# Feed-forward block of an encoder layer: block pairs gated as (i, i+11), right-operand sums of the down product made at gating, and a rebuilt buffer and load plan for the down product

## The chip, the cores and the metric

One Trainium2 chip, one core. The metric is the device time of one execution in microseconds (us). Three runs of the kernel before took 1331.19, 1335.35 and 1338.98 us; the median is 1335.35 us. The profiled execution is a run of its own, with its own time.

The engines are TensorE (PE, with its weight loads listed as PEld), VectorE (DVE), ScalarE (ACT), GpSimd (POOL) and SyncE (SP), which here only issues transfers. Each engine works through its own list of instructions in order. An instruction that waits holds up everything behind it on its engine, and a transfer that waits holds up those behind it on the queue that issues it.

## The reference, cut to what matters

The kernel computes one encoder layer on 1024 rows of width 1024: an SSD group and a chunked attention group side by side, an output projection, then a gated feed-forward part, and a last norm. The change touches the feed-forward part and the last norm:

```
h   = rmsnorm(x) * (1 + sc_f) + sh_f
u   = causal_dwconv3(h @ w_up)            # 1024 x 5632
g, v = split(u, 2)                        # 1024 x 2816 each
x   = x + g_f * ((silu(g) * v) @ w_down)  # 2816 -> 1024
out = rmsnorm(x) * final_norm_w
```

All of it is float32. The kernel splits each float32 operand into a high and a low part and multiplies three times: high by high, high by low, low by high.

## The kernel before

The 2816 channels of the feed-forward part are 22 blocks of 128. Both matrix products are done by a seven-product scheme for two by two blocks (Strassen's, in Winograd's form), which replaces eight block products by seven at the cost of sums of operands. The products are called P1, P2, P3, Q4, Q5, Q6 and Q7.

**Up product and gating.** A `Unit` (L838 to L902) is one channel block, with its g and its v half. The loop at L938 takes two units at a time, 2q and 2q+1, in 11 rounds (KH = 11). `Unit.__init__` queues the loads of its slice of `w_up` into `ya` or `xs`. `sums` (L844) makes the sums of the weights on DVE. `prep` splits two weight blocks at once through `wsplit` (L818): ACT writes the high part (L66), DVE the low part (L69), both into a buffer of a ring of five (`ring`, L810). `product` runs four steps of three matmuls (`mm3`, L55 to L58) into a PSUM bank of tag X, Y or Z, and `post` empties the bank. `conv` (L889) is the causal convolution: a scaled copy on ACT (L892) and two multiply-adds on DVE (L894). `finish` (L897) does the convolution of the g half, the silu on ACT (L900), the product on DVE (L901), and stores the gated block of 128 channels by 1024 rows into the DRAM tensor `gd`, from ACT's queue (L902).

**Down product.** The tensor `gd` is the right operand and `w_down` the left one. Each is seen as two by two blocks: channel blocks 0 to 10 and 11 to 21 (index 1 and 2), and two halves of 512 rows or columns. So `b11` is blocks 0 to 10 and rows 0 to 511, `b12` the same blocks and rows 512 to 1023, `b21` and `b22` the same halves of blocks 11 to 21; `a11` and so on are the blocks of `w_down`. Two channel blocks at a time are a "pair" m, six pairs per product, the last of one block only (`kn`, L967). `load_pair` (L970) queues a transfer of a pair on SP. `operands` (L1000) makes the sums of a product's operands on DVE through `add` (L995), ten of them for each m over the seven products. `split_pair` (L1022) splits both operands, and `step` (L1026) runs 4 times `mm3`, one for each of four tiles `st` of 128 rows: 12 matmuls for one channel block. The product P1 writes banks d, Q6 banks e, and so on; the order is P1, Q6, Q5, Q7, P3, Q4, P2.

The down stage has a pool of buffers of its own, `dp`, which is opened after those of the up stage are closed, and so lies in the memory that they held. a11, a21, a22, b11, b12 and b22 each have a buffer for each m; a12 and b21 share two buffers (tag `st`) and are loaded for each product anew. `add_x1` (L1042) fetches a tile of the residual `x1d` into one of two buffers, `gate` (L1047) multiplies by the gate row and adds it, and `final` (L1051) does the last norm of four halves of rows and the stores. The last three channel blocks of P2 are kept back and done tile by tile (L1117), so that a tile's norm can run beside the next tile's matmuls.

**What sets the order.** The program is written in one order, but a planner puts the instructions of each engine in the order in which its own model of their times makes them ready; where several are ready, the earlier written goes first. The waits between engines are put in by the framework. A buffer is handed on when all users of the tile that held it are through. The last round of the up stage (q = 10) is not finished in the loop: `finish` of its two units, blocks 20 and 21, is written after the first splits of P1 (L1064 to L1068).

Of the kernel before, what the change touches and what calls it, by code (L numbers as in the profile page):

```python
# [45 lines left out]
def tile_block(ctx: ExitStack, tc: tile.TileContext, x, crep, pk, w_ada, w_first, w_ft, w_z,  # L46
# [13 lines left out]
    def split(hi, lo, src, ehi, elo, scale=None):  # L60
        if scale is not None:
            A.activation(hi, src, AF.Copy, scale=scale)
            V.scalar_tensor_tensor(lo, src, scale, f32(hi), op0=ALU.mult, op1=ALU.subtract)
            return
        if ehi is A:
            A.activation(hi, src, AF.Copy)  # L66
        else:
            ehi.tensor_copy(hi, src)
        elo.tensor_tensor(lo, src, f32(hi), ALU.subtract)  # L69
# [645 lines left out]
    gd = dram.tile([NF, P, S], F32, name="gd")  # L715
# [55 lines left out]
    def h_new(pool, n):  # L771
        hb_[n] = [pool.tile([P, 4, 512], F32R, name=n + p) for p in "hl"]
# [45 lines left out]
    def wsplit(src, n=2):  # L818
        w = ring()[:, :, 0:n, :]
        split(w[:, 0], w[:, 1], src, A, V)  # L820
        return w

    fp_ = []
# [14 lines left out]
    class Unit:  # L838
        def __init__(self, i):
            self.i, self.b, self.ps, self.w, self.done = i, (ya, xs)[i % 2], {}, {}, set()  # L840
# [25 lines left out]
        def post(self, p, ps):  # L866
# [14 lines left out]
            elif p == "Q4":  # L881
                V.tensor_tensor(self.v[:, 0:512], ps, self.v[:, 0:512], ALU.subtract)  # L882
                self.a = a_tile()
# [13 lines left out]
        def finish(self):  # L897
# [4 lines left out]
            nc.scalar.dma_start(gd[self.i], a[:, 1, :])  # L902

    units = [Unit(0), Unit(1)]
# [7 lines left out]
    hc2 = es_h.enter_context(tc.tile_pool(name="hc2", bufs=1, side="right", reuse_waits="tile"))  # L912
    for n in ("t3", "t4", "t1", "b22", "t2"):
        h_new(hc2, n)
# [22 lines left out]

    for q in range(KH):  # L938
        if q > 0:
            units = [Unit(2 * q), Unit(2 * q + 1)]  # L940
# [4 lines left out]
        for n, p in enumerate(order):  # L945
# [5 lines left out]
            for u in units:  # L951
                u.product(p)
        if q < KH - 1:
            for u in units:
                u.finish()
    es_f.close()
    es_h.close()
    es_y.close()


    dp = ctx.enter_context(tc.tile_pool(name="dp", bufs=1, side="right", reuse_waits="tile"))
    ps4 = ctx.enter_context(tc.tile_pool(name="ps4", bufs=1, space=PSUM, reuse_waits="tile"))
    NM = (KH + 1) // 2
    res = {}
    BLK = {"11": (0, 0), "12": (0, 1), "21": (1, 0), "22": (1, 1)}

    def kn(m):  # L967
        return min(2, KH - 2 * m)

    def load_pair(n, m, tag=None):  # L970
        i, j = BLK[n[1:]]
        src = w_down if n[0] == "a" else gd
        if n[0] == "a":
            i, j = j, i
            i, j = (0, 1)[n[2] == "2"], (0, 1)[n[1] == "2"]
        k0 = i * KH + 2 * m
        t = dp.tile([P, kn(m) * 512], F32, tag=tag or f"{n}_{m}", bufs=2 if tag else 1, name=n)
        t = t.rearrange("p (k c) -> p k c", c=512)
        nc.sync.dma_start(t, src[k0:k0 + kn(m), :, halves[j]].rearrange("k p c -> p k c"))
        return t  # L980

    def res_load(names, ms=range(NM)):
        for m in ms:
            for n in names:
                res[n, m] = load_pair(n, m)

    def sm(m):
        t = dp.tile([P, 1024], F32, tag="sm", bufs=2, name="sm")[:, 0:kn(m) * 512]
        return t.rearrange("p (k c) -> p k c", c=512)

    def bank(t="d"):
        return ps4.tile([P, 512], F32, tag=t, bufs=4, name="dn")

    def add(o, a, b, op=ALU.add):
        V.tensor_tensor(o, a, b, op)  # L995
        return o

    sub = ALU.subtract

    def operands(p, m):  # L1000
        r = lambda n: res[n, m]
        if p == "P1":
            return r("a11"), r("b11")
        if p == "Q6":
            add(r("a11"), r("a11"), r("a21"))
            add(r("b11"), r("b11"), r("b12"), sub)
            return add(sm(m), r("a11"), r("a22")), add(sm(m), r("b11"), r("b22"))
        if p == "P2":
            return load_pair("a12", m, "st"), load_pair("b21", m, "st")
        if p == "Q7":  # L1010
            return r("a11"), add(r("b12"), r("b12"), r("b22"), sub)
        if p == "Q5":
            return add(r("a21"), r("a21"), r("a22")), r("b11")
        if p == "Q4":
            t = load_pair("b21", m, "st")
            add(t, t, r("b22"), sub)
            return r("a22"), add(t, t, r("b11"), sub)
        t = load_pair("a12", m, "st")
        add(t, t, r("a22"))
        return add(t, t, r("a11")), r("b22")  # L1020

    def split_pair(p, m):  # L1022
        a, b = operands(p, m)
        return wsplit(a, kn(m)), wsplit(b, kn(m))

    def step(ps, ab, k, sts, start):  # L1026
        a, b = (t[:, :, k % 2, :] for t in ab)
        for st in sts:
            c = slice(st * P, (st + 1) * P)
            mm3(ps[st], b[:, 0, c], b[:, 1, c], a[:, 0, :], a[:, 1, :], start and k == 0,  # L1030
                k == KH - 1, not start)

    def product(p, ps, start, ready=()):
        for m in range(NM):
            ab = ready[m] if m < len(ready) else split_pair(p, m)
            for k in range(2 * m, 2 * m + kn(m)):
                step(ps, ab, k, R4, start)

    def xt_():
        return dp.tile([P, 512], F32, tag="xt", bufs=2, name="xt")  # L1040

    def add_x1(t, st, dh):  # L1042
        x = xt_()
        nc.sync.dma_start(x, x1d[st * P:(st + 1) * P, halves[dh]])
        V.tensor_tensor(t, t, x, ALU.add)

    def gate(t, src, st, dh):  # L1047
# [125 lines left out]
```

## Time and profile before

| | |
|---|---|
| median of three runs | 1335.35 us (1331.19 to 1338.98) |
| profiled execution: its time, its span | 1335.92 us, 1334.2 us |
| PE busy, matmuls | 1216.5 us, 5818 |
| DVE busy, instructions | 991.9 us, 1516 |
| ACT busy, instructions | 550.1 us, 900 |
| last matmul of the up product starts | 1051.13 us |
| first matmul of the down product starts | 1063.22 us |
| last group of matmuls of the down product starts | 1317.95 us |

The profile counts a matmul as busy from its start to its modelled end, and matmuls overlap in the pipeline; so the starts tell more than the busy time. A row of a timeline gives start, duration, engine, line, operation, and output from inputs; in brackets stands the idle time of the engine before it and what ended it. A row of a group gives count, busy time and mean duration, then the idle time before its members. Rows of a table of stretches give for each engine the busy time and the count, then the granted clock of TensorE (1.00 is full speed), the share of the transfer engines and GB/s.

### The profile page before, as it was taken

Reading aid. Unit: us, or ns where it says so; the run is one execution under the profiler, and the core shown is the slowest. Engines: PE = TensorE matmul, PEld = TensorE weight load, DVE = VectorE, ACT = ScalarE, POOL = GpSimd, SP = SyncE. Lnnn points to the kernel's source line nnn. Section 1 sums busy time; section 2 is a strip of 40 time slices with the busy share of each in tenths; the row PEclk is TensorE's granted clock in tenths of the full one; section 3 lists DMA queues with packets and bytes.
Section 4 is the critical chain, followed back from the end, with each engine's and each line's share of the span. In section 5 each row is a group of like instructions: output and inputs, shape, how many; then the busy total and the mean of one; then the engine's idle time right before and its main releaser. Section 6 shows DMA issues by size and latency. Waiting matters only on the chain.

```text
span 1334.2 us, 15392 instructions
## 1 busy us (share of the span) xinstructions
PE 1216.5 (91%) x5818; PEld 995.9 (75%) x5818; DVE 991.9 (74%) x1516; ACT 550.1 (41%) x900; POOL 105.7 (8%) x114
## 2 busy tenths in 40 slices
PE   5999999999999699997799999999999696998884
PEld 4777887788788587775688888888888574886763
DVE  7727566765998877658799887877896689549875
ACT  4525554653233523237344444343344332433332
POOL 1300111001201422110000000000000000000001
PEclk9999998999999999997899999999999797998997
DMA  9601110002745221121122221222220392003264
GB/s 338 218 0 50 33 36 32 27 17 81 257 154 187 96 64 34 62 95 64 63 93 89 87 73 61 77 89 95 95 96 32 137 378 84 0 28 106 80 199 156
DMA packets 50393, 132.23 MB, mean 99 GB/s; under 512 B 4880, under 2 KB 5008, under 8 KB 50320
## 3 DMA queue, kind: packets, MB, share of 16 engines
q1 hardware_dynamic: 44848, 115.53, 25.9%
q10 hardware_dynamic: 5472, 15.73, 3.0%
q8 instruction: 45, 0.74, 0.2%
q14 instruction: 28, 0.23, 0.1%
HBM read 110.79 MB, written 20.45 MB: 98 GB/s over the span
## 4 chain that ended last, share of the span: by engine, by line
PE 67%; DVE 17%; DMA 8%; ACT 3%; issue 2%; POOL 1%; SPq 0%; DVEq 0%; ACTq 0%
PE uY L56 4%; PE uY L57 4%; PE uY L58 4%; DMA b<-gd 3%; PE dn L58 3%; PE uX L56 3%; PE dn L56 3%; PE dn L57 3%; PE uX L57 3%; PE uX L58 3%; PE acc L56 3%; PE acc L57 3%; PE uZ L57 3%; PE uZ L56 3%; PE acc L58 3%; PE uZ L58 3%
## 5 line engine op out<-in xcount | busy, mean ns | idle before, releaser
L56 PE MATMUL dn<-w 128*128 128x512 f32 x308 | 122.8, 413 | 31.4 <-ACT w L66 25.7
L57 PE MATMUL dn<-w 128*128 128x512 f32 x308 | 121.8, 410 | 1.3 <-DVE w L69 1.3
L58 PE MATMUL dn<-w 128*128 128x512 f32 x308 | 108.4, 404 | 6.9 <-DVE w L69 6.9
L56 PEld LDWEIGHTS dn<-w 128*128 128x128 f32 x308 | 61.2, 200 | 47.8 <-ACT w L66 28.8
L66 ACT ACTIVATE w<-ya 128x1024 fp32r<-128x1024 f32 (+1 forms) x44 | 41.8, 949 | 97.4 <-PE uY L58 88.9
L58 PEld LDWEIGHTS dn<-w 128*128 128x128 f32 x308 | 60.2, 197 | 22.1 <-DVE w L69 9.4
L57 PEld LDWEIGHTS dn<-w 128*128 128x128 f32 x308 | 61.4, 200 | 15.2 <-DVE w L69 2.0
L66 ACT ACTIVATE w<-b 128x1024 fp32r<-128x1024 f32 (+1 forms) x36 | 35.5, 987 | 87.5 <-PE dn L58 58.9
L69 DVE TENSOR_TENSOR w<-b,w 128x1024 fp32r<-128x1024 f32 (+1 forms) x36 | 40.8, 1132 | 40.0 <-ACT w L66 40.0
L753 POOL TENSOR_TENSOR st<-st,mhalf 128x1 f32<-128x1 f32 x16 | 11.8, 739 | 735.5 <-DVE st L752 735.3
L69 DVE TENSOR_TENSOR pt<-tp,pt 128x512 fp32r<-128x512 f32 (+2 forms) x72 | 42.2, 595 | 27.7 <-ACT pt L66 27.6
L66 ACT ACTIVATE w<-xs 128x1024 fp32r<-128x1024 f32 (+1 forms) x44 | 41.8, 950 | 40.9 <-PE uY L58 33.7
L894 DVE SCALAR_TENSOR_TENSOR a<-cv,pkt,a 128x1023 f32<-128x1023 f32 (+1 forms) x44 | 56.2, 1276 | 1.4 <-ACT a L892 1.3
L66 ACT ACTIVATE pt<-tp 128x512 fp32r<-128x512 f32 (+2 forms) x72 | 36.7, 523 | 45.0 <-PE tp L349 16.0
L56 PE MATMUL s<-hth,wh 128*128 128x512 f32 x128 | 51.4, 402 | 3.8 <-DVE ct L413 2.3
L894 DVE SCALAR_TENSOR_TENSOR a<-cg,pkt,a 128x1023 f32<-128x1023 f32 (+1 forms) x44 | 54.5, 1277 | 0.0
L882 DVE TENSOR_TENSOR cv<-uY,cv 128x512 f32<-128x512 f32 x22 | 15.1, 687 | 50.4 <-PE uY L58 50.4
L317 DVE CUSTOM_DVE_ANT_0 p<-s,bias 128x640 f32<-128x640 f32 (+4 forms) x64 | 40.3, 649 | 15.9 <-PE tp L352 7.5
L57 PE MATMUL s<-htl,wh 128*128 128x512 f32 x128 | 51.2, 400 | 0.0
L69 DVE TENSOR_TENSOR w<-ya,w 128x1024 fp32r<-128x1024 f32 (+1 forms) x44 | 47.7, 1085 | 4.4 <-ACT w L66 4.4
L58 PE MATMUL s<-hth,wl 128*128 128x512 f32 x128 | 50.8, 397 | 0.0
L69 POOL TENSOR_TENSOR wl<-raw_t,wh 128x1024 fp32r<-128x1024 f32 x14 | 35.0, 2501 | 185.9 <-ACT wh L66 152.5
(334 smaller groups left out, 3629.8 us busy)
## 6 DMA issues: line engine op xcount, KB each, us to landing
mt<-in_w_ada_dram SPq DMA_DIRECT2D x32, 512.0 KB, 4.3
a<-in_w_down_dram SPq DMA_DIRECT2D x25, 512.0 KB, 6.9
b<-gd SPq DMA_DIRECT2D x25, 512.0 KB, 5.2
gd<-a ACTq DMA_DIRECT2D x22, 512.0 KB, 3.0
ya<-in_w_up_dram SPq DMA_DIRECT2D x11, 768.0 KB, 4.1
xs<-in_w_up_dram SPq DMA_DIRECT2D x11, 768.0 KB, 4.8
adat<-in_w_ada_dram SPq DMA_DIRECT2D x16, 512.0 KB, 5.9
raw_t<-in_w_ft_dram SPq DMA_DIRECT2D x14, 512.0 KB, 3.5
```

The costliest lines, as they stand in the source:

```text
L56: T.matmul(ps, lh, rh, start=start, stop=False, skip_group_check=more)
L57: T.matmul(ps, lh, rl, start=False, stop=False, skip_group_check=more)
L58: T.matmul(ps, ll, rh, start=False, stop=stop, skip_group_check=more)
L66: A.activation(hi, src, AF.Copy)
L69: elo.tensor_tensor(lo, src, f32(hi), ALU.subtract)
L317: V.tensor_tensor_reduce(out=dst, in0=src, in1=bsl, scale=-1.0, scalar=3e38, op0=ALU.add, op1=ALU.min, accum_out=nm)
L753: G.tensor_tensor(r, ms, mhalf[:, 0:1], ALU.pow)
L882: V.tensor_tensor(self.v[:, 0:512], ps, self.v[:, 0:512], ALU.subtract)
L894: V.scalar_tensor_tensor(a[:, j:S], c[:, 0:S - j], w[2 - j], a[:, j:S], op0=ALU.mult, op1=ALU.add)
```

## The change

1. The loop takes units q and 11+q together instead of 2q and 2q+1, so that a round has one block of each half of the right operand.
2. `finish` no longer stores the whole block. For the unit of the first half, b11's part is stored ("x"). A new `store_pair` makes the four sums that the seven products need of the right operand, t1 = b11-b12, t3 = b12-b22, t2 = b22+t1 and t4 = b21-t2, by four DVE instructions of 128x512, and stores them from ACT's queue: t1 and t3 (tensor "y", 512 KB) and t2, t4, b21 and b22 (tensor "z", 1 MB).
3. The down stage has no pool of its own. Its buffers are the slots of the up product's operands (`HOME`), each handed over once the operand in it has had its last product; the right operands go round in 14 slots. A queue in the program (`queue`, `pump`) writes a load as soon as its slot's last reader is written, and every load is kept behind the load before it (`issue_after`).
4. The first two pairs of P1 are loaded and split before P3 of the last round; the emptying of P3's banks and `finish` are kept behind those splits. `finish` of block 10 comes after them, and `finish` of block 21 and the last `store_pair` after the split of P1's fourth pair (m = 3).
5. The order of products is P1, Q5, Q6, Q7, Q4, P3, P2. Every product has its own PSUM group, alternately in banks d and e. The left operand's sums are made in place: two for each m in Q5, one in Q6, one in P3. Each is kept behind the low part of the pair three places earlier.
6. `gate` and `final` use parts of `ya` and `xs`; three of the four groups of gates come right after Q6, Q7 and Q4, the fourth with the tail. The last tile's sum is made in `p1` instead of the transfer buffer.

```
+            if self.i < KH:
+                nc.scalar.dma_start(gd["x", self.i // 2][self.i % 2, :, 0], a[:, 1, 0:512])
+    def store_pair(units):
+        q, (a, c) = units[0].i, (u.a for u in units)
+        h0, h1 = halves
+        m, k = q // 2, q % 2
+        V.tensor_tensor(a[:, 0, h0], a[:, 1, h0], a[:, 1, h1], ALU.subtract)
+        V.tensor_tensor(a[:, 0, h1], a[:, 1, h1], c[:, 1, h1], ALU.subtract)
+        nc.scalar.dma_start(gd["y", m][k].rearrange("p a b -> p (a b)"), a[:, 0, :])
+        V.tensor_tensor(c[:, 0, h0], c[:, 1, h1], a[:, 0, h0], ALU.add)
+        V.tensor_tensor(c[:, 0, h1], c[:, 1, h0], c[:, 0, h0], ALU.subtract)
+        nc.scalar.dma_start(gd["z", m][k].rearrange("p a b -> p (a b)"), c.rearrange("p a b -> p (a b)"))
...
+    def load(key, m):
...
+        with tc.issue_after(last_load[0]) if last_load else ExitStack():
+            i = nc.sync.dma_start(t, src.rearrange("k p c -> p k c"))
...
+    def pump():
+        while queue and (queue[0][0] in ("a11", "a21", "a22") or sc[0] % NS not in busy):
+            n, m = queue.pop(0)
+            res[n, m] = load(n, m)
...
+    def down_first():
+        loads(("a11", "b11"), range(NM - 1))
+        loads(("a11",), (NM - 1,))
+        pre = []
+        for m in range(2):
+            a, b = res["a11", m], take("b11", m)
+            pre.append((wsplit(a), wsplit(b)))
+            los.append(last_split[1].ins)
+        return pre
...
-            units = [Unit(2 * q), Unit(2 * q + 1)]
+            units = [Unit(q), Unit(KH + q)]
...
-            for u in units:
-                u.product(p)
+            if p == "P3" and q == KH - 1:
+                pre = down_first()
+            with tc.issue_after(los[0]) if los else ExitStack():
+                for u in units:
+                    u.product(p)
...
+    def add(o, a, b):
+        with tc.issue_after(los[max(0, len(los) - 3)]):
+            V.tensor_tensor(o, a, b, ALU.add)
         return o
...
+        if p == "Q5":
+            add(a11, a11, a21)
+            add(a21, a21, a22)
+        elif p == "Q6":
+            add(a21, a11, a22)
+        elif p in ("P3", "P2"):
+            a = take("a12" + p, m)
+            if p == "P3":
+                add(a, a, a21)
...
+    def late(m):
+        if m == 3:
+            with tc.issue_after(last_split[0].ins), tc.issue_after(last_split[1].ins):
+                units[1].finish()
+                store_pair(units)
+            loads(("a21", "a22", "t1"), range(4, NM))
+            for n in ("t2", "t3", "t4"):
+                loads((n,))
+            loads(("a12P3", "b22"))
+            loads(("a12P2", "b21"))
+            nc.sync.dma_start(gf, gfd)
```

277 lines of the change are left out of this document (153 added, 124 removed).

## The prediction, made before the change was run

> **What bounds the kernel now.** I read the page first, then the stretches from the feed-forward part on, then the groups of the down product, then each engine's timeline there. The page, with TensorE's slices and clock:
>
> ```profile
> span 1334.2 us, 15392 instructions
> ...
> PE   5999999999999699997799999999999696998884
> ...
> PEclk9999998999999999997899999999999797998997
> ```
>
> TensorE is full from slice 20 to 31 and has holes after. The table of stretches says the same:
>
> ```profile
> 700.00:740.00 40.00, 40.00 (x178) 33.11 (x177) 32.04 (x38) 17.45 (x20) 0.00 (x0) 1.00 0.25 84
> 1050.00:1060.00 10.00, 1.52 (x7) 0.94 (x5) 8.78 (x9) 4.42 (x4) 0.00 (x0) 0.69 0.13 52
> 1060.00:1070.00 10.00, 6.78 (x21) 5.50 (x22) 6.53 (x6) 4.84 (x5) 0.00 (x0) 0.63 0.65 229
> 1110.00:1120.00 10.00, 6.18 (x18) 4.27 (x16) 10.00 (x12) 1.75 (x2) 0.00 (x0) 0.74 0.00 0
> 1190.00:1210.00 20.00, 14.30 (x61) 11.55 (x61) 11.85 (x14) 7.09 (x8) 0.00 (x0) 0.93 0.10 29
> 1280.00:1290.00 10.00, 6.83 (x28) 4.94 (x27) 10.00 (x15) 2.84 (x4) 0.00 (x0) 0.96 0.44 152
> ```
>
> Columns after the length: PE, PEld, DVE, ACT, POOL busy with counts, clock, share of the transfer engines, GB/s. In the gating rounds (first row) TensorE never stops and DVE is busy 32 of 40 us. From 1050 us on the stages differ: there TensorE waits, and at 1110 and 1280 us DVE is busy all the time. The down product by groups, and its first and last matmuls:
>
> ```profile
> L56 PE MATMUL dn<-w 128*128 128x512 f32 x308 | 122.8, 413 | 31.4 <-ACT w L66 25.7 <-DVE pU L1091 5.7
> L57 PE MATMUL dn<-w 128*128 128x512 f32 x308 | 121.8, 410 | 1.3 <-DVE w L69 1.3
> L58 PE MATMUL dn<-w 128*128 128x512 f32 x308 | 108.4, 404 | 6.9 <-DVE w L69 6.9
> ```
> ```profile
> 1051.13 0.39 PE L58 MATMUL uZ<-b22h,w 128*128 128x512 f32 x1
> 1063.22 0.79 PE L56 MATMUL dn<-w 128*128 128x512 f32 x1 [11.71 <-ACT w L66]
> ...
> 1317.95 1.07 PE L58 MATMUL dn<-w 128*128 128x512 f32 x4
> ```
>
> At full speed a pair (two channel blocks, 24 matmuls) takes the distance of two splits that each wait for TensorE:
>
> ```profile
> 1178.92 1.06 ACT L66 ACTIVATE w<-b 128x1024 fp32r<-128x1024 f32 x1 [3.43 <-PE dn L58]
> ...
> 1184.36 1.06 ACT L66 ACTIVATE w<-b 128x1024 fp32r<-128x1024 f32 x1 [3.43 <-PE dn L58]
> ```
>
> That is 5.44 us, 0.2267 us a matmul. The 924 matmuls need 209.4 us; from the end of the up product (1051.13 + 0.39 = 1051.5) to the end of the last group (1317.95 + 1.07 = 1319.0) pass 267.5. The excess is 58.1 us: 31.4 + 1.3 + 6.9 = 39.6 us idle, and 18.5 us of slow clock and broken spacing. This is what can be won before the tail; no matmul is added or removed (seven products of eleven blocks both times).
>
> The Trainium skill, "TensorE: Matmul & The Clock Gate", section "Back-to-back issue gap", gives N / 2.4 + 2.5 ns as the isolated warm spacing, 215.8 ns at 512 columns; by it the 924 matmuls would take 199.4 us, 10 us less. The rows above measure 226.7 ns here, with the weight loads between, and decide.
>
> **The change part by part. The start of the down stage.** The operands of P1's first pairs were in early, but their splits ran late:
>
> ```profile
> 1036.68 0.47 SPq L979 DMA_DIRECT2D a<-in_w_down_dram  x1
> ```
> ```profile
> 1060.80 0.33 ACTq L902 DMA_DIRECT2D gd<-a  x1
> 1061.17 1.06 ACT L66 ACTIVATE w<-a 128x1024 fp32r<-128x1024 f32 x1 [1.66 <-DVE a L901]
> ```
>
> ACT took the convolution, the silu and the store of the last two units first. The change writes four splits before P3 of the last round and holds the emptying of P3's banks and `finish` behind them, so the order is fixed and not left to the planner. Their ring buffers: two are free when Q7 of that round ends, two when Q4 of each unit ends, the last one P3 (5.44 us) before 1051.5, at 1046.1; a split takes about 2.3 us over both engines (1.06 and 1.22), so the last is ready 3 us ahead. The first left operands go where b11 stood, whose last product, P1 of the last round, ends six products of 5.44 us before 1051.5. I count the 11.7 us as gone, with bounds of 0 and 11.7 us left. What is late next is the third pair's right operand, whose ring buffer comes free after the first pair (1057): 3 us of margin before 1062.4, with `finish` of one unit between (three DVE instructions of some 1.2 us, like L901 below). I take 1 us.
>
> Block 10 reaches P1 through `finish`, a store and a load; the store holds the loads behind it on SP.
>
> ```profile
> gd<-a ACTq DMA_DIRECT2D x22, 512.0 KB, 3.0
> b<-gd SPq DMA_DIRECT2D x25, 512.0 KB, 5.2
> ```
>
> `finish` takes about 6 us (five instructions of 1.1 to 1.2); with 3.0 and 5.2 us block 10 is in at about 1066, and wanted at 1051.5 + 5 pairs = 1078.7. Block 21 starts behind the fourth pair's split, at about 1065 (the second pair's end, 1062.4, and 2.3); 6 us and four sums of 0.60 make 1073, the 1 MB store some 6 more. Its t1 is wanted in Q5's sixth pair, 1081.4 + 27.2 = 1108.6. Neither is waited for.
>
> **Sums of the right operand.** Consecutive starts on DVE in a full stretch:
>
> ```profile
> 1107.09 1.22 DVE L69 TENSOR_TENSOR w<-sm,w 128x1024 fp32r<-128x1024 f32 x1
> 1108.23 1.22 DVE L995 TENSOR_TENSOR b<-b,b 128x1024 f32<-128x1024 f32 x1
> 1109.36 0.68 DVE L995 TENSOR_TENSOR a<-a,a 128x512 f32<-128x512 f32 x1
> 1109.97 1.21 DVE L69 TENSOR_TENSOR w<-sm,w 128x1024 fp32r<-128x1024 f32 x1
> ```
>
> An add or split costs 1.135 us on a pair, 0.60 on a half one: 6.3 us over six pairs. The down stage had ten sums for each m, 63 us, and has four, 25 us. More weighs where they fall. Before, Q6 opened with four sums a pair, and the planner ran sums ahead of the splits: in the stretch at 1110 DVE is full and TensorE has 18 matmuls where 44 fit. After, DVE needs per pair of 5.44 us of TensorE: Q5 two sums and two splits, 4.5 us; Q6 and P3 one and two, 3.4; Q7, Q4 and P2 two splits, 2.3. All fit, and the sums are held behind the third last pair's split.
>
> The gating rounds get the four 512 sums, 4 x 0.60 = 2.4 us of DVE in a round of 7 x 24 matmuls = 38.1 us, where it had 30.5 busy by the stretch at 700 (32.04 x 38.1 / 40): now 33. One round as it is:
>
> ```profile
> 835.98 1.22 DVE L901 TENSOR_TENSOR a<-a 128x1024 f32<-128x1024 f32 x1
> ...
> 846.85 1.22 DVE L69 TENSOR_TENSOR w<-xs,w 128x1024 fp32r<-128x1024 f32 x1
> ...
> 853.00 0.69 DVE L882 TENSOR_TENSOR cv<-uY,cv 128x512 f32<-128x512 f32 x1 [4.93 <-PE uY L58]
> ```
> ```profile
> 853.96 1.14 ACT L892 ACTIVATE a<-cv,pkt 128x1024 f32<-128x1024 f32 x1
> ```
>
> The sums come after the second gated product (837.2) and push what follows by 2.4 us at most; a hole of 4.9 us takes that up at 848. I count nothing, with bounds of 0 and 2.4 us for each of ten rounds; a gain is excluded, since nothing leaves the rounds. ACT issues three stores a round instead of two (0.33 us more, ACT has over half its time free). Stored bytes rise from 1 to 1.75 MB a round, some 20 GB/s more on 84; the stretch at 1060 moved 229. The next convolution overwrites `a` at 853.96, so the 1 MB store has from 839.7 on 14 us; at 3.0 us for 512 KB it needs about 5.
>
> **Loads.** Down loads rise from 30 pairs of right operands to 42, but 14 slots hold them some 14 pairs ahead in the products with one load a pair (over 70 us) and 7 ahead in P3 and P2 (38 us). Before, two buffers a tag left P3 and P2 waiting for transfers:
>
> ```profile
> 1201.90 1.22 DVE L995 TENSOR_TENSOR a<-a,a 128x1024 f32<-128x1024 f32 x1 [3.81 <-DMA a<-in_w_down_dram]
> ```
> ```profile
> 1292.08 1.06 ACT L66 ACTIVATE w<-b 128x1024 fp32r<-128x1024 f32 x1 [2.86 <-DMA b<-gd]
> ```
>
> These are the stretches at 1190 and 1280. I count both holes gone. SP is strictly in order, so a waiting `x1d` load can hold those behind it by the few us that an add is late; the 38 us cover it.
>
> **Hand-overs.** At Q6 to Q7, Q7 to Q4, Q4 to P3 and P3 to P2, DVE empties four banks and gates, work written earlier than the next splits. Between Q7 and Q4 that is 4 evictions, 8 sums and 8 gate instructions, 20 x 0.60 = 12 us, of which some 7 us are ready at once. The ring leaves 3 us of slack: a right operand's split starts as a pair ends (1178.92), takes 2.3 us, and is wanted 5.44 later. So a hand-over costs between 0 and 7.2 - 3 = 4.2 us; I take 2 each, 8 in all. The 5.7 us that TensorE waited for L1091 (group row of L56) go: there P3 added to a bank that L1091 still had to read, and now each product has banks that were emptied a product earlier. Gates also wait for transfers:
>
> ```profile
> 1304.77 0.69 DVE L1045 TENSOR_TENSOR cv<-cv,xt 128x512 f32<-128x512 f32 x1 [2.32 <-DMA xt<-x1d]
> ```
>
> The longest such wait lies within the slack; 1 us.
>
> **Does a short hole cost more than itself?** Here two holes:
>
> ```profile
> 1064.24 0.63 PE L56 MATMUL dn<-w 128*128 128x512 f32 x1
> ```
> ```profile
> 1308.92 0.50 PE L56 MATMUL dn<-w 128*128 128x512 f32 x1 [2.02 <-ACT w L66]
> ...
> 1310.13 0.63 PE L56 MATMUL dn<-w 128*128 128x512 f32 x1
> 1310.55 0.63 PE L57 MATMUL dn<-w 128*128 128x512 f32 x1
> ```
>
> After 11.7 us idle, but also after 2.0 us (the last of several in that stage), some nine matmuls stand 0.43 us apart: 9 x 0.2 = 1.8 us more. The Trainium skill, on the same page, section "What's actually happening", lets the clock fall only after an idle window of about 3.4 us; by that rule my four short hand-overs cost nothing beyond themselves, by the row up to 7 us more. I add nothing, since each follows 27 us of full load, and keep the 7 in the range.
>
> **The tail.** From 1319.0 to the end of the span are 15.2 us. The low-part matmuls of all four tiles came last together (the x4 group), so four norms queue up on DVE: 4 x (2 x 0.60 + 0.15 + 2 x 0.74) = 11.3 us:
>
> ```profile
> L1058 DVE SCALAR_TENSOR_TENSOR fin<-xt,st,fnr 128x512 f32<-128x512 f32 x4 | 3.0, 747 | 0.1
> L752 DVE SCALAR_TENSOR_TENSOR st<-st 128x1 f32<-128x1 f32 x8 | 1.2, 156 | 1.3 <-ACT fin L1055 1.3
> ```
>
> With both last splits ready, tiles end 9 matmuls = 2.04 us apart and the queue starts 6.1 us earlier. Bounds 9 and 15.2; I take 12, since tiles 4 to 7 are normed just before on DVE.
>
> **Sum.** 1051.5 + 209.4 + 1 + 8 + 1 + 12 = 1282.9 us of span. The profiled execution took 1335.92 us for a span of 1334.2, so 1.7 us more: 1284.6, or 1285 us against 1335.92 (0.6 above the median of 1335.35). That is 51 us, 3.8%, faster.
>
> **The rivals.**
>
> 1. The start stays late: the planner or a late transfer puts P1 where it was. For it: the splits of before also stood early in the program. Against: the order is now fixed by edges. It gives 1284.6 + 10.7 + 5 of slow clock = 1300 us.
>
> 2. DVE stays the brake: blocks at the hand-overs in full, sums ahead of splits. For it: 10.00 of 10 at 1110 and 1280 us. Against: 38 us less work there. Hand-overs 17 instead of 8, 7 of slow clock, tail 15, Q5 short by 5: 1284.6 + 9 + 7 + 3 + 5 = 1309 us.
>
> 3. Slower than before: the gating rounds stretch. If the four sums fall into the hole at 848, the 1 MB store starts about 850 and ends 855 to 860, and the next convolution (853.96), which overwrites `a`, waits, with ACT and DVE behind it. It decides once the wait exceeds 5.1 us a round beyond the slack (51 us over ten rounds). At 7 us: 1284.6 + 70 = 1355 us. Against: the sums are written before the next round's, are ready at 837 and come first; 1 MB has 14 us.
>
> 4. No difference: half of 2 and half of 3 together, about 1335.
>
> **How the numbers follow.** Forecast (1271 to 1298, from 0 to full hand-overs and tails of 9 to 15) 0.73; rival 1 0.07; rival 2 0.10; rival 3 0.05; no difference 0.05. The range goes from 1271 (no hand-over cost, tail of 9 and nothing else: 1051.5 + 209.4 + 9 + 1.7) to 1312, behind rivals 1 and 2. Runs of this kernel tell about 0.5% (6.7 us) from no change: faster by more 0.90, within 0.05, slower 0.05.
>
> **What would show it.** Right: TensorE goes from P3 of the last round to the first down matmul with less than 1 us idle at about 1051; the rounds still 38.1 us; idle before down matmuls under 15 us in all; no wait of a split for a transfer; sums of the down stage 25 us; 9 to 15 us from the last matmul to the end. Wrong: rounds longer than 38.5 us, a split waiting for `gd`, a hole over 5 us at a hand-over, or a first down matmul after 1058.

## The result, and the profile after

The kernel after takes 1277.02 us (median of four runs, 1275.92 to 1280.88), the kernel before 1335.9 us beside it (median of four, 1331.19 to 1338.98): ratio 0.9567, 95% interval 0.9532 to 0.9603, so 4.3% faster where 3.8% was forecast. The profiled execution is the longest of the four, 1280.88 us. Its page, with the rows of TensorE and of its granted clock:

```profile
span 1279.2 us, 15473 instructions
...
PE   5999999999998968998789999999999999999995
...
PEclk9999999999999989999889999999999999999998
```

The digits below 9 that stood in the last quarter of both rows are gone; only the last slice, the tail, is left. The table of stretches, with the windows that were shown of before as far as they exist (columns as there):

```profile
700.00:740.00 40.00, 40.00 (x179) 33.11 (x178) 36.91 (x46) 16.93 (x19) 0.00 (x0) 1.00 0.33 121
1050.00:1060.00 10.00, 10.00 (x45) 8.29 (x45) 10.00 (x11) 4.32 (x4) 0.00 (x0) 1.00 0.62 220
...
1110.00:1120.00 10.00, 10.00 (x46) 8.29 (x45) 6.80 (x7) 5.85 (x8) 0.00 (x0) 1.00 0.54 194
1190.00:1210.00 20.00, 20.00 (x90) 16.57 (x89) 17.70 (x22) 8.77 (x14) 0.00 (x0) 1.00 0.56 177
```

TensorE is full in every stretch of the down product, at the full clock. At 1050 us VectorE is busy 10.00 of 10 us, as it was in the holes of before, and TensorE does not stop: how busy VectorE is was not the sign to go by. The groups of the down product, and its two ends on TensorE's timeline:

```profile
L56 PE MATMUL dn<-w 128*128 128x512 f32 x308 | 111.9, 389 | 0.0
L57 PE MATMUL dn<-w 128*128 128x512 f32 x308 | 111.9, 389 | 0.0
L58 PE MATMUL dn<-w 128*128 128x512 f32 x308 | 103.3, 389 | 0.0
```
```profile
1055.50 0.39 PE L58 MATMUL uZ<-b22h,w 128*128 128x512 f32 x1
1055.73 0.39 PE L56 MATMUL dn<-w 128*128 128x512 f32 x1
...
1264.94 0.39 PE L58 MATMUL dn<-w 128*128 128x512 f32 x1
```

All 924 matmuls stand without one wait: 0.0 us idle where it was 39.6, and 1264.94 + 0.39 - 1055.73 = 209.6 us for the stage, which is the 209.4 of the prediction's floor. From the end of the up product (1055.9) to the end of the last group pass 209.4 us, against 267.5 before. The profiled spans differ by 1334.2 - 1279.2 = 55.0 us: 58.1 in this stage, 1.3 in the tail (15.2 before, 1279.2 - 1265.3 = 13.9 now), and 4.4 back, since the up product ended that much later in this execution (1055.9 against 1051.5). That does not come from the gating rounds; the first matmuls of each form of the gating rounds, from before and then from after:

```profile
L56 PE MATMUL uX<-b11h,w x88: 387/389/795, 613.0 to 1018.0; 128*128 128x512 f32 x88
```
```profile
L56 PE MATMUL uX<-b11h,w x88: 389/389/796, 618.7 to 1022.4; 128*128 128x512 f32 x88
```

The rounds began 5.7 us later and took 403.7 us up to that matmul instead of 405.0. The spans of the other three runs of after are 2.9 to 5.0 us shorter, so I put the later beginning down to this one execution; what stretched it isn't settled.

### The profile page after: what moved, and what is told of

Same layout as the page of the kernel before. It is cut to its first block, busy times and chain, and to the rows that moved or that the text cites. A ratio compares the mean times of both kernels' runs of the same rounds, so it can differ in the third digit from the quotient of the medians.

```text
span 1279.2 us, 15473 instructions
## 1 busy us (share of the span) xinstructions
PE 1200.3 (94%) x5818; PEld 988.5 (77%) x5818; DVE 978.3 (76%) x1528; ACT 550.3 (43%) x904; POOL 106.5 (8%) x114
## 4 chain that ended last, share of the span: by engine, by line
PE 79%; DVE 14%; DMA 3%; ACT 2%; issue 2%; POOL 1%; SPq 0%; DVEq 0%; POOLq 0%; ACTq 0%
PE dn L57 5%; PE dn L56 5%; PE dn L58 5%; PE uY L56 5%; PE uY L58 5%; PE uY L57 5%; PE acc L56 3%; PE uZ L58 3%; PE uZ L56 3%; PE uZ L57 3%; PE acc L57 3%; PE uX L58 3%; PE uX L56 3%; PE uX L57 3%; PE acc L58 3%; PE s L302 3%
## 5 line engine op out<-in xcount | busy, mean ns | idle before, releaser
L56 PE MATMUL dn<-w 128*128 128x512 f32 x308 | 111.9, 389 | 0.0
L57 PE MATMUL dn<-w 128*128 128x512 f32 x308 | 111.9, 389 | 0.0
L58 PE MATMUL dn<-w 128*128 128x512 f32 x308 | 103.3, 389 | 0.0
L65 ACT ACTIVATE w<-ya 128x1024 fp32r<-128x1024 f32 (+1 forms) x44 | 41.8, 949 | 96.8 <-PE uY L58 88.5
L56 PEld LDWEIGHTS dn<-w 128*128 128x128 f32 x308 | 57.8, 188 | 12.1
L57 PEld LDWEIGHTS dn<-w 128*128 128x128 f32 x308 | 57.8, 188 | 12.0
L58 PEld LDWEIGHTS dn<-w 128*128 128x128 f32 x308 | 57.8, 188 | 11.9
L66 DVE TENSOR_TENSOR pt<-tp,pt 128x512 fp32r<-128x512 f32 (+2 forms) x72 | 42.2, 595 | 27.8 <-ACT pt L65 27.6
L65 ACT ACTIVATE w<-xs 128x1024 fp32r<-128x1024 f32 (+1 forms) x44 | 41.9, 951 | 42.8 <-PE uY L58 34.8
L65 ACT ACTIVATE pt<-tp 128x512 fp32r<-128x512 f32 (+2 forms) x72 | 36.7, 523 | 45.1 <-PE tp L346 16.0
L902 DVE SCALAR_TENSOR_TENSOR a<-cv,pkt,a 128x1023 f32<-128x1023 f32 (+1 forms) x40 | 51.0, 1276 | 0.0
L66 DVE TENSOR_TENSOR w<-ya,w 128x1024 fp32r<-128x1024 f32 (+1 forms) x44 | 47.7, 1085 | 4.1 <-ACT w L65 4.1
L66 POOL TENSOR_TENSOR wl<-raw_t,wh 128x1024 fp32r<-128x1024 f32 x14 | 35.0, 2502 | 186.5 <-ACT wh L65 153.1
L317 ACT ACTIVATE p<-p,st 128x640 f32<-128x640 f32 (+4 forms) x64 | 44.1, 690 | 13.0 <-DVE st L314 12.7
L902 DVE SCALAR_TENSOR_TENSOR a<-cg,pkt,a 128x1023 f32<-128x1023 f32 (+1 forms) x40 | 49.5, 1276 | 0.0
L66 DVE TENSOR_TENSOR w<-xs,w 128x1024 fp32r<-128x1024 f32 (+1 forms) x44 | 47.6, 1082 | 0.4 <-ACT w L65 0.4
L110 DVE CUSTOM_DVE_ANT_0 mt<-mt,rowa 128x1024 f32<-128x1024 f32 x32 | 40.5, 1270 | 9.6 <-DMA mt<-in_w_ada_dram 9.6
```

Source lines behind the costliest of these rows:

```text
L56: T.matmul(ps, lh, rh, start=start, stop=False, skip_group_check=more)
L57: T.matmul(ps, lh, rl, start=False, stop=False, skip_group_check=more)
L58: T.matmul(ps, ll, rh, start=False, stop=stop, skip_group_check=more)
L65: i = A.activation(hi, src, AF.Copy) if ehi is A else ehi.tensor_copy(hi, src)
L66: return i, elo.tensor_tensor(lo, src, f32(hi), ALU.subtract)
L110: V.tensor_tensor_reduce(out=t, in0=t, in1=rowa, scale=1.0, scalar=0.0, op0=ALU.mult, op1=ALU.add, accum_out=modc[:, ft:ft + 1])
```

## The experiments

The runs of one kernel lie between 1.5 and 11.8 us apart, and the intervals of the ratios reach 3 to 6 us to each side. So a difference under about 6 us between two variants is no finding by the time alone; there the profile decides. "After" is 1277.02 us; the medians of the kernel before beside the variants were 1334.68 to 1335.08 us. In order: median, TensorE's idle time before down matmuls in the profiled execution, ratio to the kernel before.

| variant | median us | idle us | ratio (95%) |
|---|---|---|---|
| after | 1277.02 | 0.0 | 0.9567 (0.9532 to 0.9603) |
| start without two of the edges | 1279.82 | 0.0 | 0.9566 (0.9534 to 0.9598) |
| first splits behind the finishing | 1289.04 | 11.2 | 0.9645 (0.9618 to 0.9672) |
| more sums, with edges | 1278.71 | 1.7 | 0.9567 (0.9537 to 0.9596) |
| sums without edges | 1286.59 | 7.1 | 0.9630 (0.9599 to 0.9661) |
| more sums, without edges | 1299.91 | 13.2 | 0.9711 (0.9666 to 0.9755) |
| four slots | 1278.67 | 0.0 | 0.9572 (0.9548 to 0.9597) |
| two slots | 1301.24 | 12.1 | 0.9749 (0.9708 to 0.9789) |
| P3 in Q4's banks | 1278.88 | 1.6 | 0.9594 (0.9560 to 0.9629) |
| more work in the gating rounds | 1277.99 | 1.6 | 0.9581 (0.9551 to 0.9612) |
| tail with buffers of its own | 1276.09 | 0.0 | 0.9540 (0.9513 to 0.9568) |
| four undoings at once | 1333.09 | 34.3 | 0.9986 (0.9963 to 1.0008) |
| before, with edges on its sums | 1315.03 | 25.8 | 0.9841 (0.9809 to 0.9873) |

### The start: without two of the edges

```
-            if p == "P3" and q == KH - 1:
-                pre = down_first()
-            with tc.issue_after(los[0]) if los else ExitStack():
-                for u in units:
-                    u.product(p)
+            for u in units:
+                u.product(p)
...
+    pre = down_first()
...
-    with tc.issue_after(last_split[0].ins), tc.issue_after(last_split[1].ins):
-        units[0].finish()
+    units[0].finish()
```

> The splits of the first half-pair of the down product are written after the loop of the up product, and the edges that held the two finishing steps and P3's products behind these splits are dropped; all buffers stay where the change put them. If the fixed order (the edges) is what closed the start gap (the prediction's reason), the gap of 11.7 us and some 5 us of slow matmuls behind it come back: about 1289 to 1294 us. If the new homes of the buffers are what freed the splits from the finishing steps, and the planner puts them early by itself, nothing changes: 1275 to 1281 us, no idle TensorE at the start of the down product.

The edit drops the edges on P3 of the last round and on `finish` of block 10. `finish` of block 21 stays in `late`, behind the fourth pair's split and with its edges, although the expectation speaks of both finishing steps.

Measured 1279.82 us, with the ratio of after, and not one wait of TensorE in the stage. ScalarE's timeline in this kernel:

```profile
1045.99 1.06 ACT L65 ACTIVATE w<-dnb11h 128x1024 fp32r<-128x1024 f32 x1 [2.12 <-PE uY L58]
1046.95 1.14 ACT L900 ACTIVATE ya<-cv,pkt 128x1024 f32<-128x1024 f32 x1
1048.71 1.06 ACT L65 ACTIVATE w<-dnt2h 128x1024 fp32r<-128x1024 f32 x1 [0.62 <-PE uY L58]
```

The planner puts these splits (L65) ahead of and between the convolutions of the last units (L900) by itself. So these two edges are not what closed the start gap, and as far as they go that reason of the prediction falls. What the late place of block 21's `finish` does for the start wasn't tried alone.

### The start: the old order

```
+    for u in units:
+        u.finish()
+    with tc.issue_after(u.end[0].ins), tc.issue_after(u.end[1].ins):
+        pre = down_first()
```

(`u.end` are the silu and the product of the last unit; the early call of `down_first` and the two later calls of `finish` go, as above.)

> Both finishing steps of the gating are written first and the splits of the first half-pair of the down product are held behind them, which is the order of the kernel before, with all else as after. If late splits are the whole start term, TensorE idles 11 to 13 us at about 1055 us and runs slower for some microseconds behind it: 1289 to 1294 us. If the start gap is worth less than that because the down stage makes it up later, under 1283 us.

Measured 1289.04 us, 12.0 more than after. TensorE's timeline:

```profile
1049.92 0.39 PE L58 MATMUL uZ<-b22h,w 128*128 128x512 f32 x1
1061.25 2.08 PE L56 MATMUL dn<-w 128*128 128x512 f32 x4 [10.95 <-ACT w L65]
```

The hole of before (11.71 us) is back with 10.95, and the stage gives nothing of it back later: from the first dn matmul to the end of the last (1272.6 + 0.39) it takes 211.8 us against 209.6. The start term is 12 us by the medians, about the lower end of the expectation. Both experiments together: what counts is that the splits run ahead of the finishing steps; in the changed kernel the planner does that with or without the two edges. Why it did not in the kernel before isn't settled: there too the first splits were written ahead of both `finish`, and the planner put them last. What the kernel without the two edges still has of the change are the new homes of the down buffers and the late `finish` of block 21; neither was undone alone, and edges on the first splits of the kernel before weren't tried.

### The sums: number and place

Four variants. More sums:

```
+    def again(t):
+        with tc.issue_after(los[max(0, len(los) - 3)]):
+            V.tensor_tensor(t, t, t, ALU.max)
...
+        for _ in range(dict(Q6=2, Q7=1, Q4=2).get(p, 0)):
+            again(b)
```

> After, with five more VectorE instructions for each pair of the down stage on the right operand (two in Q6, one in Q7, two in Q4; each takes the maximum of the operand with itself, so the values stay the same), as many as the kernel before had sums there, all held behind the split of the third-last pair: 30 at up to 1.14 us, some 31 us more. If placement decides (the prediction's 'more weighs where they fall'), the loss is 0 to 8 us: 1277 to 1285 us. If the amount of VectorE work is what braked the stage, 25 to 30 us: 1302 to 1308 us, with holes before the down matmuls in Q6 and Q4.

1278.71 us and 1.7 us idle: 30 more VectorE instructions, as many as the change took off the right operand, cost nothing that the time shows (VectorE's busy time on the page is 1008.0 us instead of 978.3). Now the edge alone:

```
-        with tc.issue_after(los[max(0, len(los) - 3)]):
-            V.tensor_tensor(o, a, b, ALU.add)
+        V.tensor_tensor(o, a, b, ALU.add)
```

> After, without the edges that hold the sums of the left operand behind the split of the third-last pair. If the edges do work of their own, the planner runs sums ahead of splits again and TensorE waits 5 to 15 us in Q5 and Q6: 1282 to 1292 us. If the smaller number of sums is enough, 1275 to 1281 us and no idle TensorE.

1286.59 us, 9.6 more. And both, with `again` without its edge too:

> The five more VectorE instructions a pair and no edges: as many sums as the kernel before and in an order left to the planner. If number and placement together make the holes of the kernel before at about 1110 us, the hole comes back around the opening of Q6 and again in Q4: 10 to 30 us idle, 1287 to 1307 us. If the spare time of VectorE per pair is enough in any order, under 1285 us.

1299.91 us, 22.9 more. TensorE's holes lie between 1064 and 1136 us, from P1 to the beginning of Q6; in Q4, where the expectation had holes too, there is none. VectorE's timeline around one of the holes of this last kernel, and TensorE behind it:

```profile
1091.05 1.21 DVE L1078 TENSOR_TENSOR dnb21h<-dnb21h,dnb21l 128x1024 f32<-128x1024 f32 x1
1092.18 0.68 DVE L918 TENSOR_TENSOR ya<-ya,xs 128x512 f32<-128x512 f32 x1
...
1093.99 1.21 DVE L1078 TENSOR_TENSOR dnt1h<-dnb11h,dnt1l 128x1024 f32<-128x1024 f32 x1
1095.12 1.21 DVE L66 TENSOR_TENSOR w<-dnt3h,w 128x1024 fp32r<-128x1024 f32 x1
```
```profile
1096.39 2.07 PE L58 MATMUL dn<-w 128*128 128x512 f32 x4 [3.10 <-DVE w L66]
```

The split for which TensorE waits (L66) starts only at 1095.12, after five sums in a row from 1091.05 on: two of the last store (L918, L920) and three of the down stage (L1078), of which `dnb21h` belongs to the last pairs, which are wanted much later. In after, the same stretch alternates:

```profile
1084.66 1.21 DVE L1079 TENSOR_TENSOR dnt3l<-dnt3l,dnb22h 128x1024 f32<-128x1024 f32 x1
1085.80 1.21 DVE L66 TENSOR_TENSOR w<-dnt3h,w 128x1024 fp32r<-128x1024 f32 x1
1086.93 1.21 DVE L1079 TENSOR_TENSOR dnb11l<-dnb11l,dnt3l 128x1024 f32<-128x1024 f32 x1
1088.07 1.21 DVE L66 TENSOR_TENSOR w<-dnt1h,w 128x1024 fp32r<-128x1024 f32 x1
```

The counter-test in the kernel before, with its ten sums a pair and only the edge added:

```
+        with tc.issue_after(los[max(0, len(los) - 3)]):
+            V.tensor_tensor(o, a, b, op)
...
+        los.append(last_split[1].ins)
```

> The kernel before, with its sums in the down stage held behind the split of the third-last pair and nothing else changed. If the order of sums and splits was a term of its own, part of the 16.8 us of holes between 1090 and 1130 us goes: 1320 to 1328 us against 1335. If the number of sums (ten for each pair) is what counts, no gain: 1330 to 1338 us.

1315.03 us, 20.1 below the 1335.08 of before beside it, and beyond the expectation. Its groups:

```profile
L56 PE MATMUL dn<-w 128*128 128x512 f32 x308 | 118.7, 403 | 24.0 <-ACT w L65 18.2 <-DVE pU L1093 5.7
L57 PE MATMUL dn<-w 128*128 128x512 f32 x308 | 117.0, 397 | 0.0
L58 PE MATMUL dn<-w 128*128 128x512 f32 x308 | 105.9, 396 | 1.9 <-DVE w L66 1.9
```

The waits for VectorE's half of the splits shrink from 8.2 to 1.9 us and those for ScalarE's from 25.7 to 18.2. From the end of the up product to the last down matmul pass 244.8 us instead of 267.5. Place is a term of about 20 us. The number matters only where the place is left open: 9.6 us without the edge, 22.9 with five more a pair.

This run also shows what else before waited for, since the edge leaves it in. Of the 25.8 us of idle, 11.71 are the start and 5.71 the bank at P3. Another 3.3 lie in Q4, where a split waits for one of VectorE's sums, and 4.6 in P2: 3.1 at three splits that had waited for transfers, 1.5 at one whose low half VectorE makes behind gates. The same places in before have 11.7, 5.7, 3.5 and 7.4 us (4.7 and 2.7 of them), beside 11.2 in Q6, where the edge leaves 0.6.

### The loads: four slots and two

```
-    NS, RM = 14, range(NM)
+    NS, RM = 4, range(NM)
```

(and the three left operands are looked up when they are there.)

> Four slots for loaded operands of the down product in place of fourteen, so that loads run at most a few steps ahead. If the depth of the loads is a term of its own (the holes of the kernel before at about 1190 and 1280 us that ended on a transfer, 6.1 and 11.3 us), it loses between 6 and 17 us: 1283 to 1294 us. If four slots already hide the transfers, or the order of VectorE's work was the cause of these holes, 1275 to 1280 us.

1278.67 us, no idle TensorE: four slots do all that fourteen do. Then two slots for all but b11 and t1:

```
+    def slot_of(n):
+        return sc[0] % 12 if n in ("b11", "t1") else 12 + sc[1] % 2
...
-            slot = sc[0] % NS
+            slot = slot_of(n)
```

> After, with two slots in place of fourteen for all right operands after Q5 and for both operands of P3 and P2 (b11 and t1 keep the rest), which is the depth that the kernel before had in P3 and P2: one pair's operands at a time. Four slots had cost nothing. If the depth of the loads is a term (prediction: the holes at 1190 and 1280), TensorE waits behind splits that wait for transfers in P3 and P2, 5 to 17 us: 1282 to 1294 us. If VectorE's and ScalarE's order made these holes, 1275 to 1281 us.

1301.24 us, 24.2 more, above the expectation. SyncE's queue and ScalarE's waits in it:

```profile
1239.46 0.37 SPq L1005 DMA_DIRECT2D dna<-in_w_down_dram  x1
...
1247.13 0.37 SPq L1005 DMA_DIRECT2D dna<-in_w_down_dram  x1
...
1267.77 0.33 SPq L1005 DMA_DIRECT2D dna<-gz  x1
1268.15 6.57 SPq L1135 DMA_DIRECT2D xs<-x1d  x4
```
```profile
1236.81 1.06 ACT L65 ACTIVATE w<-dna 128x1024 fp32r<-128x1024 f32 x1 [3.71 <-DMA dna<-in_w_down_dram]
...
1244.79 1.06 ACT L65 ACTIVATE w<-dna 128x1024 fp32r<-128x1024 f32 x1 [5.30 <-DMA dna<-in_w_down_dram]
```

With one pair in flight in P3 and P2, a load is issued (1239.46) after the split before it has freed the slot, and the next split waits for it (till 1244.79). The rest lies in the tail, 21.9 us instead of 13.9 (the last down matmul starts at 1275.0 of 1297.3): SyncE works in order, and the four `x1d` loads for the last gates stand behind the last late load (1268.15). So the depth is a term, it sits between two slots and four, and it has a second price behind the queue. It is not the depth of the kernel before in all of P3 and P2, as the expectation says: there P3 and Q4 load one operand a pair into the two buffers, and only P2 loads both. So 24.2 us is not the size of before's own term; the 4.7 us at late transfers in P2 above, and what a late load adds to the hole at P3 (under "Hand-overs" below), are nearer to that.

### The banks

```
-    Z = banks("e")
+    Z = banks("d")
     product("P3", Z)
-    W = banks("d")
+    W = banks("e")
```

> After, with P3 in the four banks that Q4 has just filled and P2 in the other four, so that P3's first matmul has to wait until VectorE has emptied Q4's first bank. The kernel before waited 5.7 us at such a place. If the banks are a term of their own, TensorE idles 2 to 6 us between Q4 and P3: 1279 to 1283 us, visible in the profile and hardly in the median. If VectorE empties the banks as TensorE goes from row tile to row tile, under 1 us.

1278.88 us; by the time no finding. TensorE's timeline:

```profile
1201.47 0.47 PE L56 MATMUL dn<-w 128*128 128x512 f32 x1 [1.56 <-DVE dnt4h L1197]
```

1.56 us where the kernel before waited 5.7: between the two expectations. The wait for a bank is real and small if VectorE reaches the eviction soon.

### More work in the gating rounds

```
+        for _ in range(2):
+            V.tensor_tensor(a[:, 0, :], a[:, 0, :], a[:, 0, :], ALU.max)
...
+        for _ in range(2):
+            V.tensor_tensor(c[:, 0, :], c[:, 0, :], c[:, 0, :], ALU.max)
```

> After, with two more VectorE instructions on the half operands ahead of each of the first two sums of a gating round (each the maximum of an operand with itself; the values stay the same): 4.5 us more VectorE work a round, ahead of the stores, in ten rounds of 38.1 us that have about 33 us. If the cover of the prediction is real (spare VectorE time of 5 us a round), 0 to 5 us in all: 1277 to 1282 us. If the later store of the gated blocks holds up the next convolution, or if VectorE is the next bound of the rounds, 2 to 4.5 us a round: 1297 to 1322 us.

1277.99 us. The stretch at 700 us:

```profile
700.00:740.00 40.00, 40.00 (x179) 33.12 (x177) 39.00 (x46) 17.04 (x19) 0.00 (x0) 1.00 0.30 105
```

VectorE is busy 39.00 of 40 us (32.04 before, 36.91 after) and TensorE still never stops. The four sums of the change and 4.5 us more go into cover that is really there, and the store that leaves later holds up nothing.

### The tail

```
+        if p == "P2" and m == NM - 1:
+            wx = hc2.tile([P, 2, 2, 512], F32R, tag="t1h", bufs=1, name="wx")
...
-        t = fins[st % 3]
+        t = buf("a22_0") if st == 3 else fins[st % 3]
```

> The operands of the last half-pair get a buffer of their own for their split, in place of one of the ring that is still being read, and the fourth output tile a buffer of its own, in place of the first tile's. The tail after the last matmul's start was 13.9 us in the profiled run of after. If the tail is set by the late split (four tiles end at once) and by the wait for the first tile's store, it shrinks to 9 to 11 us: 1272 to 1274 us. If it is set by the stores themselves, no change: 1276 to 1278 us.

1276.09 us (six runs): 0.9 below after, not to be told from it, so by the time the second expectation came. The profile tells more. VectorE after the last down matmuls, first in after, then here:

```profile
1258.83 0.68 DVE L66 TENSOR_TENSOR w<-dna,w 128x512 fp32r<-128x512 f32 x1
1264.23 1.29 DVE L1213 TENSOR_TENSOR xs<-dn,ya 128x512 f32<-128x512 f32 x2 [4.72 <-PE dn L58]
```
```profile
1260.17 0.69 DVE L1219 TENSOR_TENSOR xs<-dn,ya 128x512 f32<-128x512 f32 x1 [3.19 <-PE dn L58]
...
1261.76 0.69 DVE L1219 TENSOR_TENSOR xs<-dn,ya 128x512 f32<-128x512 f32 x1 [0.17 <-PE dn L58]
```

With the split ready earlier the first tile is taken up at 1260.17, 4.7 us before the last matmul's end (1264.9), and the tail is 1276.1 - 1264.9 = 11.2 us instead of 13.9. The 2.7 us stand in the trace and drown in the spread. The edit gives two buffers at once, one to the split and one to the fourth tile; what each does alone wasn't tried.

### Four undoings at once

The old order at the start, more sums without edges, two slots and P3 in Q4's banks, each with the edit above.

> Four undoings at once in after: splits of the first half-pair behind the finishing steps, five more VectorE instructions a pair in the order of the planner, two slots for the later operands, P3 in the banks of Q4. By the sum of the single effects measured, 1277 + 12 + 22 = 1311 us plus what the slots and the banks cost by themselves (0 to 17 and 1 to 6): 1312 to 1334 us. If it comes near the 1335 us of before, the account is closed with these four; if it stays under 1310, the effects overlap; the rest would lie in what these four leave out.

1333.09 us, ratio 0.9986 (0.9963 to 1.0008): the time of before. Single: 12.0 + 22.9 + 24.2 + 1.9 = 61.0 us; together 1333.09 - 1277.02 = 56.1. But it is not the loss of before again. Two stretches, first of the kernel with more sums and no edges alone, then of this one:

```profile
1055.00:1140.00 85.00, 71.67 (x278) 55.92 (x277) 77.51 (x77) 30.45 (x36) 0.00 (x0) 0.90 0.53 189
```
```profile
1062.00:1160.00 98.00, 97.95 (x426) 80.65 (x425) 80.61 (x80) 38.79 (x45) 0.00 (x0) 0.99 0.37 127
```

Alone, the sums without edges open all their holes in the first of these stretches (13.2 us of waits). Here TensorE has no wait in the second, though the sums are the same. All of its waits but the start's 10.9 us come after 1160 us: 23.3 us, where the two-slot kernel by itself has 12.1. Before has 11.2 us of waits in Q6, where this kernel has none. From the end of the up product to the last down matmul pass 257.7 us (267.5 in before), and the tail takes 22.0 us (15.2). So the four are not separate, and that the time comes out at before's is in part luck: 9.8 us too few in the stage and 6.8 too many behind it. Why the sums' holes moved isn't settled. What of before's loss is shown is what the runs of single parts show: the start, the place of the sums, the bank, and the late loads of P2. What is left in of the change (the sums made in the rounds, the order of the products, the larger stores) was not undone, and this run doesn't show that it gains nothing.

## Why the prediction was right, and where not

**The excess.** The sum rested on a floor of 209.4 us for the 924 matmuls and an excess of 58.1 us that could go. Both hold: the stage takes 209.4 to 209.6 us, and all 58.1 us are gone. The low end of the range was built on this case with a tail of 9 us; the stage came so, the tail did not.

**The start.** One microsecond was left; none is. The reason given, that "the order is fixed and not left to the planner", failed in part: without the edges on P3 and on block 10 the time is the same. The edges on block 21 were never dropped. Rival 1, the late start, priced at 10.7 + 5 us, is worth 12.0 when it is forced; its 5 us of slow clock were too many, 211.8 - 209.6 = 2.2 is what the stage shows.

**The sums.** "More weighs where they fall" is shown: about 20 us by place (the kernel before with the edge), nothing by number with the edge. The 38 us of VectorE time saved, which stood as the argument against rival 2, were no argument by themselves: the 30 us of them put back behind the edge change nothing that the time shows. The edge was the argument, and without both the loss is 22.9 us.

**Loads.** That the holes at 1190 and 1280 us would go was right, but four slots are enough, not fourteen. The stretches that the prediction read the term from miss 5.7 and 3.2 us of TensorE's time. The first hole is only in part a late load's (next point). TensorE's timeline of before in the second:

```profile
1287.88 1.20 PE L58 MATMUL dn<-w 128*128 128x512 f32 x4 [2.67 <-DVE w L69]
```

So 2.67 of its 3.2 us end at the low half of a split that VectorE makes at 1286.61, behind eight steps of gates (L1045, L1048), though ScalarE began the high half at 1281.98. That is VectorE's order and no transfer, and behind the row at 1292.08 that the prediction quotes TensorE does not stop. Late transfers cost before 4.7 us of idle in P2, and 3.1 with the edges on its sums. The 24.2 us of the two-slot kernel are the price of a plan that is shallower than before's in P3.

**Hand-overs.** The term that was wrong in size: 8 us taken, 0 measured. The prediction put the evictions and gates in a block ahead of the next splits, "work written earlier than the next splits". VectorE's timeline of after shows them mixed:

```profile
1196.36 1.21 DVE L1079 TENSOR_TENSOR dnt3h<-dnt3h,dnt1h 128x1024 f32<-128x1024 f32 x1
1197.49 0.68 DVE L66 TENSOR_TENSOR w<-dnb21l,w 128x512 fp32r<-128x512 f32 x1
1198.09 0.68 DVE L1133 TENSOR_TENSOR ya<-ya,xs 128x512 f32<-128x512 f32 x1
1198.70 0.68 DVE L66 TENSOR_TENSOR w<-dnt2h,w 128x512 fp32r<-128x512 f32 x1
...
1206.22 0.68 DVE L1197 TENSOR_TENSOR dnt4h<-dnt4h,dn 128x512 f32<-128x512 f32 x1
```

The planner puts a gate (L1133) or an eviction (L1197) between splits (L66). That the product's own banks allow this, since nothing has to be emptied at once, is argued and not shown. For the banks the 5.7 us did go, but the step named half the cause. Set back alone the shared banks cost 1.56 us. VectorE's timeline of before, right behind the sum at 1201.90 that the prediction quotes:

```profile
1203.04 0.68 DVE L1090 TENSOR_TENSOR pU<-dn,cg 128x512 f32<-128x512 f32 x1
...
1208.24 0.68 DVE L1091 TENSOR_TENSOR pU<-pU,dn 128x512 f32<-128x512 f32 x1
```

That sum had waited 3.81 us for a transfer, and the evictions (L1090, L1091) that free the bank stand behind it. The prediction had shown the same sum under the loads: it was one hole, with a late load as its beginning and the shared bank as its end, and it was told of twice (the sum took the excess as a whole and did not count it twice). Without the 3.81 us the bank alone would be some 5.7 - 3.8 = 1.9 us, by estimate, near the 1.56 above.

**The x1d waits.** One microsecond taken, none lost.

**The rounds.** No cost, as counted; with 4.5 us more a round still none. Rival 3 does not decide even there.

**The tail.** 12 us taken, 13.9 measured, inside the bounds. The step assumed both last splits ready. In after the last one waits for a ring buffer and then behind the finals of tiles 4 to 7 on VectorE (1258.83 in the fence above), so the four tiles end together again, as before; with a buffer of its own it is 11.2.

Together: 1284.6 - 8 - 1 - 1 + 1.9 + 4.4 = 1280.9 us, against 1280.88 for the profiled execution; the median lies 3.9 below that.

## What to carry to other kernels

Ask of each engine that feeds the bound one which of its instructions run ahead of the one that is waited for: an edge that holds work without a deadline behind the split with one was worth 20 us here, and 30 us less work behind the same edge was worth nothing that could be seen. A prefetch depth can be enough all at once: here two pairs in flight cost nothing and one pair 24 us, and what queues behind the late load pays too. And when all parts are undone at once, compare where the time is lost, and not only how much: here the total came back to the old time with the holes in other places.

## What the runs showed of the hardware that was not expected

A hole of TensorE of about 3 us can be followed by a lower granted clock, and shorter ones mostly are not. The stretches of the two-slot kernel, where holes of several lengths stand alone (2.92 us of idle before 1213.16, 1.72 before 1228.00, 3.08 before 1239.54, 1.44 before 1254.37):

```profile
1210.00:1220.00 10.00, 7.08 (x25) 5.56 (x24) 5.07 (x5) 3.57 (x4) 0.00 (x0) 0.83 0.31 108
1220.00:1230.00 10.00, 8.19 (x36) 6.12 (x35) 5.47 (x5) 2.62 (x3) 0.00 (x0) 1.00 0.38 124
1230.00:1240.00 10.00, 6.92 (x31) 5.44 (x30) 6.26 (x10) 3.38 (x4) 0.00 (x0) 1.00 0.41 139
1240.00:1250.00 10.00, 9.82 (x36) 7.27 (x35) 5.43 (x7) 2.12 (x2) 0.00 (x0) 0.83 0.49 153
1250.00:1260.00 10.00, 8.56 (x37) 6.51 (x36) 3.67 (x3) 3.90 (x4) 0.00 (x0) 1.00 0.48 163
```

After the holes of 2.9 and 3.1 us the ten-microsecond mean falls to 0.83, after those of 1.4 and 1.7 us it stays at 1.00. Over the 4 us right behind them the clock is 0.58 and 0.61 after the two longer holes. The length alone does not decide: in the kernel with four undoings the clock was 0.57 over the 4 us after a hole of 1.79 us, and 1.00 after one of 2.96. A fall of 0.17 over 10 us is 1.7 us more for such a hole. The Trainium skill, "TensorE: Matmul & The Clock Gate", section "What's actually happening", puts the fall behind at least one idle window of about 3.4 us on a free-running count. Here idle stretches below that length were enough, so the measurement decides. The lower clock is part of why 12.1 us of waits cost the two-slot kernel 18.9 us in the stage (228.5 us from its first to its last matmul, against 209.6).
